# Where a store is written in ScalarE's order: behind its root, or behind the next load's square

## The chip, the cores and the metric

The kernel runs on one core of one Trainium2 chip. The metric is the device time of one execution in microseconds (us). A run is called fast when it shows no sign of the chip's slower state (a lower clock or a time over 1.5% above the fastest of its kernel). One transfer queue belongs to SyncE (SPq), one to ScalarE (ACTq); ScalarE is ACT in the profile, VectorE is DVE.

## The reference, cut to what matters

```python
x: (32, 256, 4096) float32, p = 2, kernel_size = 4
window = np.abs(x[:, :, start:start + 4]) ** p
result[:, :, i] = np.mean(window, axis=-1) ** (1.0 / p)     # (32, 256, 1024)
```

So: square, sum in fours, divide by four, root. 134.2 MB are read and 33.6 MB written, with next to no arithmetic.

## The kernel before

Three input tiles of 128 x 13184 elements take turns, and two output tiles of 128 x 6592. ScalarE squares a load in place, VectorE sums it in fours into half of an output tile, and once both halves of a group (two loads) are there, ScalarE roots it in place and the tile is stored. SyncE issues the loads, numbered from 0; a load waits until the sum has freed its input tile. ScalarE issues the stores of groups 0 to 6; those of groups 7 to 10 wait at the end of SyncE's queue, behind all loads, to fill the transfer engines at the end.

```python
def root(g, o, ends):
    r = nc.scalar.activation(out=o, in_=o, func=Act.Sqrt, scale=1.0 / k)
    ...
    if ends and g not in late:
        store(g, nc.scalar)                     # right behind its root
...
for i in range(n):                              # one load each
    ...                                         # issue loads whose tile is free
    for step in chunks:
        ...
            r = nc.scalar.activation(out=v, in_=v, func=Act.Square)
        ...
        total_sum(ots[g][:, summed:summed + step // k], v, i)     # VectorE
        while pending and pending[0][0] <= done - LAGS.get(pending[0][1], 1):
            root(*pending.pop(0)[1:])           # one square later than its last sum
        ...
```

A group is rooted one square late, so that ScalarE need not wait for the sum: square 3, square 4, root of group 1 (loads 2 and 3), store, square 5, square 6, root of group 2, store.

## Time and profile before

| | before |
|---|---|
| time, median of 6 runs | 394.45 us (393.62 to 395.62) |
| span in the profile | 393.3 us |
| ScalarE, VectorE busy | 70%, 70% |
| bytes moved, mean rate | 167.77 MB, 427 GB/s |

The runs fall in two clusters, 393.6 to 394.1 and 394.8 to 395.6, so a difference of half a per cent means nothing here.

### The profile page before, as it was taken

The page shows a single profiled execution, that of the slowest core. Times are in us where ns is not written, and L with a number is a line of the kernel's source. Part 1 is how long each engine was busy: PE and PEld are TensorE (multiplying, and loading weights), DVE is VectorE, ACT ScalarE, POOL GpSimd, SP SyncE. Part 2 cuts the span into 40 slices and gives each one's busy share as a digit, 9 for nine tenths or more (in the row PEclk, how much of TensorE's full clock was granted, in tenths as well). Part 3 has the DMA queues.
Part 4 walks back from the last instruction along what each step waited for, and adds up shares of the span by engine and source line. Part 5 has one row for each costly group of instructions (what it writes and reads, how often), then busy time and mean ns, then how long its engine had stood idle before and what let it go on. Part 6 is the DMA issues. An engine that isn't in the chain of part 4 may idle for free.

```text
span 393.3 us, 182 instructions
## 1 busy us (share of the span) xinstructions
DVE 274.5 (70%) x36; ACT 275.4 (70%) x38; POOL 0.2 (0%) x4
## 2 busy tenths in 40 slices
DVE  4207898885869376948693869396929690989991
ACT  1095879919990899099809991998099809986991
POOL 0000000000000000000000000000000000000000
DMA  8999999999989999999999999999999899999996
GB/s 312 429 440 429 467 445 451 381 432 469 434 386 429 472 429 429 456 402 429 429 432 426 429 472 429 456 400 467 429 437 429 386 429 467 429 429 423 440 409 295
DMA packets 4554, 167.77 MB, mean 427 GB/s; under 512 B 526, under 2 KB 526, under 8 KB 556
## 3 DMA queue, kind: packets, MB, share of 16 engines
q1 hardware_dynamic: 3501, 144.04, 85.0%
q10 hardware_dynamic: 1053, 23.73, 14.0%
HBM read 134.22 MB, written 33.55 MB: 427 GB/s over the span
## 4 chain that ended last, share of the span: by engine, by line
DMA 54%; ACT 25%; DVE 19%; SPq 0%; issue 0%; ACTq 0%
DMA xt<-in_x_dram 54%; ACT xt L167 22%; DVE ot L111 14%; DVE xt L122 3%; ACT ot L102 3%; DVE ot L124 1%; DVE xt L124 1%; ACT xt L102 1%; SPq L82 0%; ACTq L99 0%; SPq L132 0%
## 5 line engine op out<-in xcount | busy, mean ns | idle before, releaser
L167 ACT ACTIVATE xt<-xt 128x13184 f32<-128x13184 f32 (+4 forms) x23 | 217.4, 9458 | 97.9 <-DMA xt<-in_x_dram 96.2
L111 DVE TENSOR_REDUCE ot<-xt 128x3296 f32<-128x13184 f32 x15 | 208.3, 13886 | 88.7 <-ACT xt L167 88.7
L102 ACT ACTIVATE ot<-ot 128x6592 f32<-128x6592 f32 x9 | 51.1, 5679 | 0.0
L122 DVE TENSOR_TENSOR xt<-xt 128x3296 f32<-128x3296 f32 (+5 forms) x9 | 34.5, 3834 | 16.9 <-ACT xt L167 16.8
L124 DVE TENSOR_TENSOR ot<-xt 128x3296 f32<-128x3296 f32 (+1 forms) x4 | 10.9, 2733 | 0.1
L143 ACT ACTIVATE ot<-ot 30x896 f32<-30x896 f32 x1 | 0.9, 948 | 10.8 <-DVE ot L139 10.8
L137 DVE TENSOR_TENSOR ot<-ot 30x3584 f32<-30x3584 f32 x1 | 3.9, 3880 | 5.0 <-DMA ot<-in_x_dram 5.0
L124 DVE TENSOR_TENSOR xt<-xt 128x1448 f32<-128x1448 f32 (+4 forms) x5 | 7.0, 1409 | 0.2
L102 ACT ACTIVATE xt<-xt 128x3296 f32<-128x3296 f32 (+3 forms) x4 | 5.8, 1445 | 1.1 <-DVE xt L124 1.1
L164 DVE TENSOR_TENSOR xt<-xt 128x5792 f32<-128x5792 f32 x1 | 6.2, 6184 | 0.0
L139 DVE TENSOR_REDUCE ot<-ot 30x896 f32<-30x3584 f32 x1 | 3.9, 3874 | 0.0
L143 ACT ACT_TABLE_LOAD x1 | 1.3, 1283 | 0.7 <-PEq L200 0.7
L200 POOL MEMSET const-bfloat16-1.0<- 128x1 bf16 x1 | 0.1, 101 | 0.0
L200 POOL MEMSET const-uint8-127<- 128x1 uint8 x1 | 0.1, 101 | 0.0
L200 POOL MEMSET const-float32-0.0<- 128x1 f32 x1 | 0.1, 98 | 0.2 <-issue 0.2
L200 POOL MEMSET const-float32-1.0<- 128x1 f32 x1 | 0.1, 98 | 0.0
## 6 DMA issues: line engine op xcount, KB each, us to landing
xt<-in_x_dram SPq DMA_DIRECT2D x19, 6592.0 KB, 31.6
out_dram<-ot ACTq DMA_DIRECT2D x7, 3296.0 KB, 27.4
out_dram<-ot SPq DMA_DIRECT2D x2, 3296.0 KB, 24.0
xt<-in_x_dram SPq DMA_DIRECT2D x1, 5404.0 KB, 24.1
out_dram<-xt SPq DMA_DIRECT2D x1, 1648.0 KB, 11.0
out_dram<-xt SPq DMA_DIRECT2D x1, 1351.0 KB, 6.6
ot<-in_x_dram SPq DMA_DIRECT2D x1, 420.0 KB, 4.2
out_dram<-ot ACTq DMA_DIRECT2D x1, 105.0 KB, 8.7
```

Of the source, the lines that this page charges most:

```text
L102: r = nc.scalar.activation(out=o, in_=o, func=Act.Sqrt, scale=1.0 / k)
L111: r = nc.vector.tensor_reduce(out=o, in_=v.rearrange("p (n j) -> p n j", j=k), axis=mybir.AxisListType.X, op=add,)
L122: r = nc.vector.tensor_tensor(out=h, in0=q[:, :, 0:2], in1=q[:, :, 2:4], op=add)
L124: r = nc.vector.tensor_tensor(out=o, in0=h[:, :, 0], in1=h[:, :, 1], op=add)
L137: nc.vector.tensor_tensor(out=t, in0=t, in1=t, op=mybir.AluOpType.mult)
L139: nc.vector.tensor_reduce(out=o, in_=t.rearrange("p (n j) -> p n j", j=k), axis=mybir.AxisListType.X, op=mybir.AluOpType.add,)
L143: nc.scalar.activation(out=o, in_=o, func=Act.Sqrt, scale=1.0 / k)
L164: r = nc.vector.tensor_tensor(out=v, in0=v, in1=v, op=mybir.AluOpType.mult)
L167: r = nc.scalar.activation(out=v, in_=v, func=Act.Square)
L200: nc = _bacc.Bacc("TRN2", target_bir_lowering=False, num_devices=1)
```

## The change

Its intent: a store's issue takes ScalarE's sequencer 0.34 us, and in four of seven places the next square stood ready and waited for it. Written behind that square, the issue can go while the square runs.

```diff
         if ends and g not in late:
-            store(g, nc.scalar)
+            held.append(g)
...
+    held = []
...
             total_sum(ots[g][:, summed:summed + step // k], v, i)
+
+            while held:
+                store(held.pop(), nc.scalar)
             while pending and pending[0][0] <= done - LAGS.get(pending[0][1], 1):
```

## The prediction

> **What bounds the kernel now.** I read the page first, its totals, its forty slices and its DMA line:
>
> ```profile
> span 393.3 us, 182 instructions
> DVE 274.5 (70%) x36; ACT 275.4 (70%) x38; POOL 0.2 (0%) x4
> DMA  8999999999989999999999999999999899999996
> DMA packets 4554, 167.77 MB, mean 427 GB/s; under 512 B 526, under 2 KB 526, under 8 KB 556
> ```
>
> Both compute engines are idle 30% of the time; the DMA row is at 8 or 9 in every slice but the last. Whether 9 means "full" is asked of the timeline of ScalarE, early on, when no store is in flight and each square only waits for its load:
>
> ```profile
> 36.18 11.19 ACT L167 ACTIVATE xt<-xt 128x13184 f32<-128x13184 f32 x1 [4.39 <-DMA xt<-in_x_dram]
> 51.76 11.19 ACT L167 ACTIVATE xt<-xt 128x13184 f32<-128x13184 f32 x1 [4.39 <-DMA xt<-in_x_dram]
> 62.85 5.68 ACT L102 ACTIVATE ot<-ot 128x6592 f32<-128x6592 f32 x1
> 68.56 0.37 ACTq L99 DMA_DIRECT2D out_dram<-ot  x1
> 68.98 11.19 ACT L167 ACTIVATE xt<-xt 128x13184 f32<-128x13184 f32 x1 [0.45 <-ACT ot L102]
> ...
> 99.95 5.68 ACT L102 ACTIVATE ot<-ot 128x6592 f32<-128x6592 f32 x1
> 105.66 0.34 ACTq L99 DMA_DIRECT2D out_dram<-ot  x1
> 106.57 11.19 ACT L167 ACTIVATE xt<-xt 128x13184 f32<-128x13184 f32 x1 [0.94 <-DMA xt<-in_x_dram]
> 129.02 11.19 ACT L167 ACTIVATE xt<-xt 128x13184 f32<-128x13184 f32 x1 [11.26 <-DMA xt<-in_x_dram]
> ```
>
> Columns: start, duration, engine, line, what; in brackets the idle time before and what ended it. Two loads of 6592 KB (6.750 MB) land 51.76 - 36.18 = 15.58 us apart, which is 433.3 GB/s. At that rate all 167.77 MB take 387.2 us, of a span of 393.3: only 6.1 us in the whole execution are not bulk transfer at full rate, and start and end must lie in them.
>
> The steady state agrees. A pair of loads and its store are 2 x 6.750 + 3.375 = 16.876 MB, or 38.95 us at 433.3 GB/s. In the same timeline the squares that wait for an even load start at 129.02 (above) and, five pairs later, at 323.68: 194.66 / 5 = 38.93 us a pair. ScalarE needs per pair 2 x 11.19 + 5.68 + 0.34 = 28.4 us, VectorE 2 x 13.89 = 27.8. So **the byte rate of the DMA engines is the bound**, and both compute engines follow it.
>
> Next the chain of waits, one round of it, because it seems to say otherwise (start, us, what):
>
> ```profile
> 140.21 5.59 ACT ot L102
> 145.81 0.02 issue
> 145.83 0.34 ACTq L99
> 146.17 0.05 issue
> 146.21 11.20 ACT xt L167
> 157.41 0.02 issue
> 157.44 13.90 DVE ot L111
> 171.33 0.02 issue
> 171.35 35.45 DMA xt<-in_x_dram
> ```
>
> It runs root, store issue, square, sum, next load, and so puts the store's issue on the path. But the load issued at 171.3 takes 35.45 us where a load takes 15.58 alone: it is queued behind the load before it. That one was issued at 154.2 and landed 30.2 us later (from the view of the load line in single windows), at 184.4. So the new load was issued 13 us before the DMA engines could begin on it. An issue that comes earlier, or up to 13 us later, changes nothing in when the bytes move.
>
> **What the Trainium skill says.** "DMA: Bandwidth & Descriptors", section "Where 436 GB/s comes from", puts the ceiling of the sixteen ports at 435.2 GB/s; the 433.3 measured above is 99.6% of it, so the trace agrees that there is nothing to gain in rate.
>
> The same page, "Queues, rings and completion order", has each DMA engine take turns between queues packet by packet. Load rows are 52,736 B and store rows 26,368 B, so a store beside a load should get a third of the rate and take 3.375 / (433.3 / 3) = 23.4 us (an estimate). The trace has 26.2 to 28.3 us for the seven large stores of the ScalarE queue, against 7.8 alone: it agrees, with some 3 to 5 us for start and end.
>
> "Perfetto Trace Analysis", section "Per-engine timelines", says for ScalarE and VectorE that an instruction is handed to a wait queue, after which the sequencer goes on to the next, and that a DMA is waited for and issued by the sequencer itself. This decides what the change does: is a store written behind a square issued when the square starts, or when it ends? VectorE's sequencer answers in this trace: a sum that waits for two things is preceded by a separate semaphore wait. The view of that line in the window 62 to 64 us:
>
> ```profile
> L111 DVEq EVENT_SEMAPHORE  x1: 21/21/21, 63.0 to 63.0; - x1
> ```
>
> At 63.0 VectorE is at the start of a sum that runs from 62.98 to 76.86 (timeline of VectorE). So the sequencer goes on while the sum runs. Nor did it go on earlier, though what it asks for, the odd store, had landed at 13.76 + 8.7 = 22.5: it passes an instruction that has started, not one still waiting.
>
> **The change part by part.** Nothing is removed or added: the orders of instructions set side by side show the same 47 rows on ScalarE, with 7 stores moved behind one square each; the four late stores on the other queue stay. The built program has each store wait for the count of its root (5 for the first, where the square behind is 6), not for the square. One store gets a second wait, on a transfer of eight issues before, long done.
>
> - *When the store goes.* By the reading above: once the next square has started and the root has ended. For the stores at 68.56, 145.83, 223.62 and 301.45 the next load had landed by then, so they are issued within 0.1 us of where they were. For those at 105.66, 183.74 and 261.57 the load lands 0.6 to 0.9 us later, so they go that much later. Sum of delays: 0.9 + 0.7 + 0.7 = 2.3 us over three stores, each with slack (next bullet).
> - *What a store's delay could hold up.* Only the sum that reuses its output tile. Store two lands at 131.8 (the same semaphore row, window 131 to 133); the sum that needs the tile starts at 140.24. Slack 8.4 us; for the first store 100.07 - 96.9 = 3.2.
> - *What ScalarE gains.* The issue (0.34 us and its gaps) no longer stands between root and square. The list of waits sums it:
>
> ```profile
> ACT xt L167 <- DMA xt<-in_x_dram: 96.2, 16, 11.3
> ACT xt L167 <- ACT ot L102: 1.7, 4, 0.4
> ```
>
> Four squares start 0.4 us earlier, and perhaps another 0.1 by overlapping the root's end, as neighbours do elsewhere (62.85 against 62.95): 4 x 0.5 = 2.0 us. The other three wait for their load and gain nothing.
> - *What of it reaches the end.* The four sums and the four load issues behind them come 0.5 us earlier, into a queue that is 13 us ahead: 0. The last load still lands when the bytes before it have moved. From its square at 369.77 the tail is unchanged: four stores on the other queue, 9.82 MB, 22.7 us at 433.3, to about 392.4. They were always behind the last load.
>
> Sum: 0 us. I take the median before, 394.8, and lean 0.1 towards the gain of ScalarE: **394.7 us**.
>
> **The rivals.**
>
> 1. *The chain is right, the square's hold is on the path.* It passes the store's issue twice (68.56, 145.83), so some 1 us, at most 2.0 us: 392.8 to 393.8. The 13 us of queued load speak against it. Even the extreme, all 6.1 us gone, is 1.6%, so faster by over 2% is closed by the bytes.
> 2. *The store goes at the square's end.* Then seven stores come 11.3 to 12.1 us later, past the slacks of 8.4 and 3.2 us, and a new wait appears: sums on VectorE waiting for the tile's store, some 4 us each, in six pairs. If it adds up, 6 x 4 = 24 us: 419. Against it: the semaphore row at 63.0, the wait on the root's count, and that 4 us are still under the 13 of queued load. If the load queue ran dry all the same, the store then in flight would use the engines. So even here I expect 395 to 397.
> 3. *Moved overlap changes the rate.* Stores share with the same kind of loads as before and the number of bytes is the same; mixed pairs ran at 38.93 us, the pure rate. No effect seen.
>
> **Range and chances.** Three runs before spread 393.62 to 395.62, 0.5%. Around 394.7 I take 393.2 to 396.4: below it lies rival 1 at its largest, above it rival 2. Faster by over 2% 0.01; slower 0.02, rival 2 with waits that add up; within 2% 0.97.
>
> **What would show it.** In the changed timeline of ScalarE: store issues at 68.6, about 106.5 and 145.8, each at its square's start, and squares that follow the root without the 0.4 us. In the waits: the row of 1.7 us gone or near nothing, and no VectorE sum waiting for a store. In the slices: the same 9s, 427 GB/s, last load landed near 369.8. I am wrong in mechanism if stores are issued near 80.2 and 117.8, and wrong in time if the DMA row has new 8s.

## More of the kernel before

The prediction shows the lines of the page, the timeline and the chain. I add one view: busy time by stretch, for two neighbouring pairs of loads and for five pairs (columns: stretch, length, busy time and count of VectorE, ScalarE and GpSimd, clock, DMA share, GB/s).

```profile
129.02:166.93 37.91, 26.04 (x3) 27.96 (x3) 0.00 (x0) 1.00 1.00 433
166.93:206.82 39.89, 29.46 (x3) 27.96 (x4) 0.00 (x0) 1.00 1.00 434
129.02:323.68 194.66, 138.21 (x12) 139.82 (x15) 0.00 (x0) 1.00 1.01 435
```

The rate is the same full 433 to 435 GB/s in each, and the compute engines are busy 28 of some 39 us.

## The result, and the profile after

| | before | after |
|---|---|---|
| median | 394.45 us | 394.22 us (393.67 to 394.77) |
| ratio, 95% interval | | 0.999 (0.9967 to 1.0013) |
| span in the profile | 393.3 us | 392.0 us |
| ScalarE, VectorE busy | 70%, 70% | 70%, 70% |
| mean rate | 427 GB/s | 428 GB/s |

The time is the same. Ratios here and below are the ratios of fast runs, with their 95% interval; they are not quite the ratio of the medians beside them. The profiled spans differ by 1.3 us, which lies inside the spread of the runs.

The timeline of ScalarE after the change, the same stretch as in the prediction and one pair more:

```profile
62.62 5.68 ACT L102 ACTIVATE ot<-ot 128x6592 f32<-128x6592 f32 x1
68.20 11.17 ACT L168 ACTIVATE xt<-xt 128x13184 f32<-128x13184 f32 x1
68.33 0.37 ACTq L99 DMA_DIRECT2D out_dram<-ot  x1
...
99.86 5.68 ACT L102 ACTIVATE ot<-ot 128x6592 f32<-128x6592 f32 x1
106.54 11.19 ACT L168 ACTIVATE xt<-xt 128x13184 f32<-128x13184 f32 x1 [1.00 <-DMA xt<-in_x_dram]
106.61 0.34 ACTq L99 DMA_DIRECT2D out_dram<-ot  x1
```

The store is issued at the start of its square, not 11 us later at its end. The first square no longer leaves a gap behind the root. The second pair shows what ordering by the sequencer means: the root ends at 99.86 + 5.68 = 105.54, but the square in front of the store waits for its load until 106.54, and the store goes only then.

Who waited for whom, after:

```profile
ACT xt L168 <- DMA xt<-in_x_dram: 97.0, 19, 10.3
DVE ot L111 <- ACT xt L168: 88.0, 15, 19.1
```

The row of squares that were held behind a root's store (1.7 us before) is gone. But the squares' waits for loads went up from 96.2 to 97.0 us, and their number from 16 to 19: ScalarE came earlier to loads that did not. Its idle time fell by 0.9 us, and the time did not follow. No sum waits for a store.

The same two stretches as before, one pair and five pairs:

```profile
127.98:166.90 38.92, 27.76 (x3) 27.96 (x3) 0.00 (x0) 1.00 1.00 434
127.98:322.59 194.61, 138.82 (x12) 139.83 (x16) 0.00 (x0) 1.00 1.00 434
```

194.61 / 5 = 38.92 us a pair, against 38.93 before and 38.95 computed from the bytes. Only the rhythm differs: before, pairs took 37.91 and 39.89 in turn, now all take 38.9. Before, a store was issued now just ahead of a load's landing (105.66, load at 106.5), now just after one (145.83), and shared its time with a different load; now it is always issued at a landing. That reading fits both traces, but no run isolates it.

### The profile page after: what moved, and what is told of

Same layout as the page of the kernel before. It is cut to its first block, busy times and chain, and to the rows that moved or that the text cites. A ratio compares the mean times of both kernels' runs of the same rounds, so it can differ in the third digit from the quotient of the medians.

```text
span 392.0 us, 183 instructions
## 1 busy us (share of the span) xinstructions
DVE 274.5 (70%) x36; ACT 275.3 (70%) x38; POOL 0.2 (0%) x4
## 2 busy tenths in 40 slices
DMA packets 4554, 167.77 MB, mean 428 GB/s; under 512 B 526, under 2 KB 526, under 8 KB 556
## 3 DMA queue, kind: packets, MB, share of 16 engines
q10 hardware_dynamic: 1053, 23.73, 14.1%
## 4 chain that ended last, share of the span: by engine, by line
DMA 56%; DVE 22%; ACT 19%; SPq 0%; issue 0%
DMA xt<-in_x_dram 56%; ACT xt L168 19%; DVE ot L111 18%; DVE xt L122 3%; DVE ot L124 1%; DVE xt L124 1%; ACT xt L102 1%; SPq L132 0%; SPq L82 0%
## 6 DMA issues: line engine op xcount, KB each, us to landing
out_dram<-ot ACTq DMA_DIRECT2D x7, 3296.0 KB, 27.2
out_dram<-ot ACTq DMA_DIRECT2D x1, 105.0 KB, 7.1
```

## The experiments

The first four ran on one chip beside 11 runs of before (median 393.91), the last three on another beside 7 (median 394.95).

**1. The change again, in five rounds.** No edit. It asks whether the small gain of the rival that believes the chain is there at all.

> The change as it stands, in five rounds, to narrow rival 1 of the prediction (the store's issue between root and square is on the path). Theory (the DMA engines' byte rate is the bound, the load queue is some 13 us ahead): ratio to before between 0.998 and 1.002, about 394.4 us. Rival 1: the held squares are on the path, 1 to 2 us of gain, ratio 0.995 to 0.9975, steadily below 1 in every round.

Measured: 394.09 us, ratio 1.0004 (0.9989 to 1.0019). A gain of 1 to 2 us would be a ratio of 0.9975 or less, which is outside: the interval leaves room for 0.4 us at most. The rival, which asks for 1 us or more, falls: the 0.4 us in front of four squares were not on the path.

**2. The store truly at the square's end.** The last 64 columns of a root are rooted behind the square, and the store needs them.

```diff
+        split = ends and g not in late
+        cut = o.shape[1] - (64 if split else 0)
+        sqrt(o[:, 0:cut])
+        if split:
+            held.append((g, o[:, cut:]))
...
-                store(held.pop(), nc.scalar)
+                hg, rest = held.pop()
+                sqrt(rest)
+                store(hg, nc.scalar)
```

> The store really goes at the end of the next square: the last 64 of a root's 6592 columns are rooted behind the square, and the store needs them. Both theories: stores issued near 79.8 and 118 us instead of 68.3 and 106.6, landing some 11.5 us later, and VectorE's first sum of a pair (it reuses the tile) waits for the store and starts near 143 to 145 instead of 139.2. Theory (queued loads absorb it): the load queue's lead falls from 13 to about 3.6 us in every second load and never to zero; 394 to 396.5 us, ratio 0.998 to 1.005. Rival 2 of the prediction (the waits add up, 6 x 4 us): near 415 to 419.

Measured: 394.25 us, ratio 1.0008 (0.9993 to 1.0024). ScalarE's timeline, then who waited:

```profile
68.45 11.17 ACT L173 ACTIVATE xt<-xt 128x13184 f32<-128x13184 f32 x1
79.53 0.24 ACT L109 ACTIVATE ot<-ot 128x64 f32<-128x64 f32 x1
79.80 0.37 ACTq L99 DMA_DIRECT2D out_dram<-ot  x1
```

```profile
DVE ot L116 <- DMA out_dram<-ot: 62.7, 6, 14.0
DVE ot L116 <- ACT xt L173: 27.7, 6, 19.0
DVE ot L129 <- DMA out_dram<-ot: 4.2, 1, 4.2
```

Stores go 11.1 to 11.5 us later, as expected, and a new wait stands in the list: VectorE's sums and additions wait 62.7 + 4.2 = 66.9 us for stores to leave the output tile, in seven places. The time does not move. Much of that wait took the place of waits for squares (88.0 to 27.7), and the rest is taken up by the queue of loads. Call lead the time by which load 7 is issued before load 6 lands. The change has 127.98 - 113.9 = 14.1 us (the square that waits for load 6, against the issue of load 7). Here load 7 is issued at 120.5, and load 6, issued at 93.6, is awaited by the square that starts at 122.95 (29.4 us from issue to landing): the lead is 2.4 us, and that was enough. The issue came only 6.6 us later than in the change, but the lead fell by 11.7, for load 6 lands 5 us sooner: the second store is issued at 117.75 instead of 106.61 and takes less of load 6's time.

**3. The square in front of the store split in two.** It asks what lets a store pass.

```diff
-                r = nc.scalar.activation(out=v, in_=v, func=Act.Square)
+                for part in ([v[:, 0:W // 2], v[:, W // 2:]] if held else [v]):
+                    r = nc.scalar.activation(out=part, in_=part, func=Act.Square)
```

> The square in front of each store is split in two halves; the second half waits for nothing but its turn on the engine. What lets a store pass the square? Reading A (the sequencer is free as soon as the instruction in front has what it waits for): stores stay within 0.1 us of the start of the first half, about 68.3, 106.6, 145.5. Reading B (the instruction in front must have started on the engine): stores go at the start of the second half, 5.6 us later, about 73.9, 112.1, 151.0. The time is the same within 0.5% in both, since 5.6 us lie inside the tile's slack of 5.4 to 8 us or nearly so.

Measured: 394.15 us in one run. The timeline:

```profile
68.67 5.68 ACT L169 ACTIVATE xt<-xt 128x6592 f32<-128x6592 f32 x1
68.80 0.37 ACTq L99 DMA_DIRECT2D out_dram<-ot  x1
74.26 5.68 ACT L169 ACTIVATE xt<-xt 128x6592 f32<-128x6592 f32 x1
```

The store is issued before the second half starts, though it is written behind it; the same at 106.56 and 145.43. Reading A holds in this run: what stands in front must have what it waits for, and need not have started.

**4. The store behind the second square.** That square waits for a load some 20 us off, and the sum behind it needs the very tile that the store reads. (The store is also written ahead of that sum, or it would send the next group's sums.)

```diff
-            held.append(g)
+            held.append((done + 1, g))
...                                     # cut: the next root keeps its declared order behind that store
+            while held and held[0][0] < done:          # ahead of total_sum
+                store(held.pop(0)[1], nc.scalar)
```

The diff is cut, and shown against the change; no root waits for a store in this run's list of waits.

> The store is written behind the second square after its root, which waits for a load that is some 20 us off. Both theories of the queue: the store goes when that square starts, about 20 us later than in the change, and the sum behind that square needs the tile the store is reading, so it waits for the store's landing, some 13 to 16 us each. My estimate from stepping both DMA queues with the traced durations: the lead of the load queue falls to about zero (-0.3 to 3.6 us), the DMA engines go idle about 8 us in all, 398 to 402 us, ratio 1.01 to 1.02. Rival (a store in flight always fills the engines, so a dry load queue costs nothing): 394 to 396, ratio under 1.005. Rival (each of seven waits of 14 us adds up): above 440.

Measured: 405.37 us, ratio 1.0285 (1.0269 to 1.0301): 3 us over my range, and both rivals are wrong. Busy time by stretch, around the landing of load 6:

```profile
118.00:122.00 4.00, 4.00 (x1) 0.13 (x1) 0.00 (x0) 1.00 0.49 211
122.00:126.00 4.00, 4.00 (x2) 4.00 (x1) 0.00 (x0) 1.00 0.99 422
```

Load 6, issued at 93.6, landed 28.3 us later, at 121.9; load 7 was issued at 124.2, so the lead is -2.3 us, and the rate drops to half in that stretch, without a surplus in the next. The same happens around 204 and 286. Each dry spell leaves some 2 us with nothing moved, 5 to 6 of the 405.37 - 393.91 = 11.5 us. The rest is no gap: the pair from 121.87 to 163.95 has a DMA share of 1.01 at 421 GB/s where the change has 1.00 at 434, so the bytes around the dry spells were slower as well. The packets in the trace (one row of a tile each) agree: those of loads took 1.97 us on average against 1.95 in the change, those of stores 1.007 against 0.978, in all some 5 us more on each of the 16 engines; the slow ones lie just behind the dry spells, at 127 to 129, 208 to 213 and 290 to 292 us. Why, stays open; that it comes with the dry queue is all that the traces show. "A store in flight fills the engines" failed because of the order: the store waits for the square, the square for the landing, and so it was issued at 121.88, when the load queue was already empty. My range was worked out with some 8 us of idle engines and the durations traced before; the idle time was no more than that, so the miss lies in the slower bytes.

**5. One extra pass on ScalarE.** The change, with a copy over the tile, in place, in front of each of the seven roots.

```diff
+        if g < 7:
+            for _ in range(1):
+                r = nc.scalar.activation(out=o, in_=o, func=Act.Copy)
```

> The change, with one extra copy pass of ScalarE over the tile in front of each of the seven roots: 5.7 us more on ScalarE in each pair, 34.1 of the pair's 38.9 us. Theory (bound by bytes, ScalarE has room and the load queue leads by 13 us): 394 to 396 us, ratio 0.998 to 1.005; the lead falls to 7 to 13 us. Rival 1 (the chain through root, store, square, sum and load issue is on the path): at least the two to seven visits of 5.7 us, 405 to 434.

Measured: 394.17 us, ratio 0.9983 (0.9968 to 0.9998). The page's line of busy times:

```profile
DVE 274.5 (70%) x36; ACT 314.6 (80%) x45; POOL 0.2 (0%) x4
```

ScalarE's busy time rose from 275.3 to 314.6 us, and none of the 39.3 us shows. Load 7 is issued at 116.5, load 6 lands at 99.5 + 26.4 = 125.9: a lead of 9.4 us. The change took a hold of 0.4 us out of ScalarE's way in four places; this run put 5.6 us into it in seven.

**6. Two extra passes.** The same with `range(2)`.

> Two extra copy passes in front of each of the seven roots: ScalarE then needs 28.1 + 11.4 = 39.5 us in a pair, just over the 38.95 us of the bytes, and its waits for sums and loads come on top. Theory: the bound moves to ScalarE and the load queue runs dry in every second load; stepping both queues with the traced durations gives a pair of 41.7 us, 405 to 412 us, ratio 1.03 to 1.045, with DMA idle 16 us more. If the path were elsewhere and ScalarE had more room than its 28 us suggest: 395. If each extra pass were paid in full: 7 x 11.4 = 80 us, 474.

Measured: 415.59 us, ratio 1.0529 (1.0511 to 1.0546). The bound moved, as expected, and further: 3.6 us over my range of 405 to 412. One pair, in the timelines of VectorE and ScalarE and by stretch:

```profile
133.32 13.89 DVE L116 TENSOR_REDUCE ot<-xt 128x3296 f32<-128x13184 f32 x1 [12.43 <-ACT xt L173]
147.24 11.42 ACT L104 ACTIVATE ot<-ot 128x6592 f32<-128x6592 f32 x2 [2.88 <-DVE ot L116]
```

```profile
122.11:164.29 42.18, 27.77 (x2) 39.24 (x6) 0.00 (x0) 1.00 0.98 399
```

A pair takes 42.18 us, of which ScalarE works 39.24 and waits 2.88 for a sum. The round closes within the compute engines: square (11.17), its sum (13.89), two copies and the root (17.1), next square. From 79.93 to 333.03 no square waits for a load. These are six pairs, and 6 x (42.18 - 38.92) = 19.6 us, of 20.6 measured over before; my estimate had 41.7 a pair. What I expected of the queue did not come: it was to run dry in every second load and leave the engines idle 16 us more. The share of 0.98 leaves 0.8 us of a pair, some 5 us in six. Load 6 lands at 105.0 + 19.2 = 124.2, and load 7 was issued before that:

```profile
L82 SPq DMA_DIRECT2D xt<-in_x_dram x1: 328/328/328, 120.9 to 120.9; - x1
```

The lead is 3.3 us, and it stays between 1.1 and 4.7 from load 6 to load 17. So a lead above zero doesn't make a kernel as fast as its bytes. And the page's row of slices for this kernel is a warning:

```profile
DMA  9999999999999989999999999999999999999997
```

It looks fuller than that of before, at 399 GB/s in the pair. A share of 0.98 at 399 GB/s against 1.00 at 434 means that a byte kept its engine busy some 7% longer (0.98 / 399 over 1.00 / 434). In the trace, load packets took 2.04 us on average against 1.95 in the change, the slow ones around the landings; why, no run here shows. The rate told the difference, the digit did not.

**7. Half of each of the seven stores.** The change, with a wrong result: half of those columns are never written (the page has 155.96 MB moved, for 167.77). All compute stays.

```diff
+        half = slice(0, columns[g] // k // 2) if g < 7 else slice(None)
-        stores[g] = queue.dma_start(out=block(of, g, k), in_=ots[g])
+        stores[g] = queue.dma_start(out=block(of, g, k)[:, half], in_=ots[g][:, half])
```

> Wrong result on purpose: each of the seven stores writes only half of its columns, so 7 x 1.6875 = 11.8 MB are not moved; every compute instruction stays. Theory (bytes are the bound): 11.8 MB at 433.3 GB/s = 27.3 us less, 366 to 369 us, ratio 0.928 to 0.936. Rival (the chain of computation is the bound, stores are hidden beside it): 392 to 395.

Measured: 366.65 us, ratio 0.9285 (0.9271 to 0.9299). Before had a median of 394.95 on that chip, so 28.3 us went, for 27.3 computed from the bytes. The rival is excluded: bytes are the bound.

The runs by the lead of load 7 over the landing of load 6:

| kernel | lead | time |
|---|---|---|
| the change | 14.1 us | 394.1 us |
| one extra pass | 9.4 us | 394.2 us |
| store at the square's end | 2.4 us | 394.3 us |
| store behind two squares | -2.3 us | 405.4 us |
| two extra passes (compute round of 42.2 us a pair) | 3.3 us | 415.6 us |

While the compute engines' own round is shorter than the 38.9 us that a pair's bytes take, the lead separates the runs: 2.4 us was enough, -2.3 was not, and nothing was tried between. Where that round is longer, as with two passes, a positive lead doesn't help.

## Why the prediction was right, and where its steps were off

**The bound** was read right: seven half stores less cost what their bytes cost, and 39.3 us more of ScalarE cost nothing.

**When the store goes** was read right from VectorE's one semaphore row: 68.33, 106.61 and 145.48 were measured, where the prediction has 68.6, about 106.5 and 145.8 (that trace began some 0.25 us earlier, by its first square at 20.36 instead of 20.60). The prediction's wording, "once the next square has started", was too strict: in the split square, work that waits only for its turn is passed before it starts. And its count was low: it took three squares to wait for their load, with delays of 2.3 us; six did, by 0.7 to 1.1 us each, 4.6 us from the roots' ends to the stores. All stayed within the slack.

**What ScalarE gains** was too large: 2.0 us predicted, 0.9 us less idle time measured. The held squares did vanish, but the squares met loads that had not landed. It made no difference to the time.

**The 13 us of lead** carried the argument, and for the change the runs bear it out. Its allowance, "up to 13 us later, changes nothing", was too generous where the store moves as well: behind two squares load 7 was issued 10.3 us later (124.2 against 113.9) and the queue ran dry all the same, because load 6, with less of a store beside it, landed 6.1 us sooner (121.9 against 128.0).

**The estimate of 23.4 us for a store beside loads** was called in agreement with the 26.2 to 28.3 us of the trace, the other 3 to 5 us being start and end. The packets divide it otherwise: for the store issued at 184.38 after the change, the first packet starts 4.9 us after the issue, 20.0 us pass from there to the end of the last, and the landing follows 2.3 us later. That the parts add up to about the same is luck; the forecast of 0 us doesn't rest on it.

**Rival 1**, the chain, fell to the five rounds. A chain that follows a load from issue to landing (35.45 us there, where a load takes 15.58 alone) cannot tell queueing from moving.

**Rival 2**, the store at the square's end, was not what the change did. As a hypothesis it was sized wrongly: "some 4 us each, in six pairs" were 66.9 us in seven places. The prediction compared the old and the new start of a sum; a wait counts from the moment VectorE is idle, and the square behind it now came earlier too. It did not matter, as the prediction also argued: 394.25 against the 395 to 397 named.

**One supporting argument does not hold in general:** "If the load queue ran dry all the same, the store then in flight would use the engines". With the store behind two squares nothing was in flight when the queue ran dry, since the store waited for the landing of the last load in it.

**One tell was badly chosen:** new 8s in the slices. The changed kernel's row has five against three, and the repeat of the same kernel has three, at the same time. Both traces even show this, in the same stretch (the lines are the changed kernel's):

```profile
76.00:80.00 4.00, 1.22 (x2) 3.38 (x1) 0.00 (x0) 1.00 1.22 527
80.00:84.00 4.00, 4.00 (x1) 0.00 (x0) 0.00 (x0) 1.00 0.75 323
```

A share of 1.22 and 527 GB/s followed by 323 average 425: a load packet, 1.95 us on average in this trace, is booked whole in the stretch where it starts. Short slices say nothing of a per cent; the mean over whole pairs does.

## What to carry to other kernels

When transfers are the bound, ask two things of a change on another engine: whether the round of compute stays shorter than the transfers of the same work (here 42.2 us against 38.9 was too long), and by how much a new load is still issued before the one ahead of it lands. With both in order, waits of 66.9 us appeared here without a change in time, at a lead of 2.4 us. Work out that lead anew with the change in place: moving a store moves the landings too. Compute the time of the bytes first; here it left 6 us of 393 to be won by anything that moves the same bytes. And check what a piece of work in flight would hide behind: a store that waits for the landing of the last queued load fills no gap before it.

## What the Trainium skill lacked or had wrong

- "Perfetto Trace Analysis", section "Per-engine timelines": its table has the sequencer free for the next instruction once one is pushed to the wait queue (T2), ahead of the moment its semaphores are satisfied (T3). Here a store behind a square that waited for its load was not issued when it could have been (root ended at 105.54) but at 106.61, with the square's start at 106.54; the next one went at 145.48, for a root that ended at 144.76, with the square's start at 145.47. It did pass a square that waited only for its turn on the engine (68.80, against a start at 74.26). So in these runs the order of waits was kept, and only the work was passed.
- "DMA: Bandwidth & Descriptors", section "Where 436 GB/s comes from": it says that for transfers between HBM and SBUF the HBM side (about 358 GB/s, a stack's rate divided by two cores) binds. As it stands that does not hold for a core alone, and the section itself goes on with a measured 425 GB/s. This core, with no other in the program, moved 434 GB/s over 194.61 us, next to the section's 435.2.
- The same page, section "Queues, rings and completion order": it has the engines switch queues by packet, and leaves out what follows for rows of unequal length. Here stores with rows half as long as the loads' took 27.2 us in most pairs, 20.0 of them from first packet to last, where the bytes alone would take 7.8 at the full rate.
- "Perfetto Trace Analysis", section "Identifying the Most-Contended Engine", advises to go by bandwidth since the occupancy of sixteen engines misleads. It has that right but gives no case; here is one: a share of 0.98 at 399 GB/s, against 1.00 at 434.
